# Layer norm on one TensorE-bound core: means, root and reciprocal on 128 columns in four groups of rows, spread by a selector

## The chip, the cores and the metric

The kernel runs on one core of a Trainium2 chip. The core has a matrix engine (TensorE, PE in the profile, with its weight loads as PEld), a vector engine (VectorE, DVE), a scalar engine (ScalarE, ACT), a general engine (GpSimd, POOL) and an engine that issues most of the transfers (SyncE, SP). Each engine works off its own instructions in order and waits on semaphores for the others. The metric is the device time of one execution in microseconds (us), lower being better.

## The reference, cut to what matters

A two-layer network over 1024 latent tokens and 1024 channels. Layer 0 has a convolution branch and a recurrent branch that share one input and one output projection. The convolution branch ends in a layer norm over the channels of each token, a SiLU, and a product with a gate:

```python
def layernorm(x, g, b):
    mu = jnp.mean(xf, axis=-1, keepdims=True)
    var = jnp.mean(jnp.square(xf - mu), axis=-1, keepdims=True)
    y = (xf - mu) * lax.rsqrt(var + LN_EPS) * g + b
...
def conformer_conv(va, vg, p):
    u = va * jax.nn.sigmoid(vg)
    u = depthwise_conv(u, p["conv_w"], p["conv_b"], CONV_PAD)
    return jax.nn.silu(layernorm(u, p["ln_g"], p["ln_b"]))
...
    y_a = conformer_conv(va, vg, p) * jax.nn.silu(ga)
    y_b, hT = rglru_branch(xb, p, h0, True)
    y_b = y_b * jax.nn.silu(gb)
    return jnp.concatenate([y_a, y_b], axis=-1) @ p["w_out"], hT
```

The matrices are float32, and the result is to be near float32.

## The kernel before, in words

Everything is stored transposed: channels on the 128 partitions in 8 tiles (`KT`), tokens along the free dimension in two halves `h` of 512 columns (`H`). A float32 matrix product is made from three products of a reduced format (`F32R`): each operand is split into a high part (a ScalarE cast) and a remainder (a subtraction on VectorE or GpSimd), and high x high, high x low and low x high are added in PSUM. One half of one 128-row weight tile is therefore 8 x 3 = 24 products of 128x128 by 128x512. `mm3_fixed` issues them as eight steps of three.

In layer 0 up to the end of the gate products the order on each engine is written out by hand: `on(engine, ...)` ties every instruction to the one before it on the same engine, through the helpers `act`, `cast` (both ScalarE), `vec` (VectorE) and `gp` (GpSimd). All of these show up in the profile under line 670, so groups are told apart by tile names there. What comes after `fixed[0] = False` is put in order by a planner, by estimated times and priorities.

The part around the change, in program order:

- The convolution runs on VectorE as a generator, whose steps `fill(n)` hands out between other work. `ln_sums` adds each finished channel tile of its result `us[j]` into `lnacc[h]`, so that afterwards only the sum over the 128 partitions is missing.
- The loop over `m` (8 weight tiles of the recurrent branch's output projection, tiles `wob`) issues the 24 products of each half, then the layer norm's work that is due there, then `wob_evict`: a ScalarE scaling out of PSUM, a sum on GpSimd and a store.
- At (m, h) = (6, 0), behind its products, the rest of the convolution is issued, `mean_parts` splits `lnacc` of both halves (128x512), and `mean` multiplies both parts by a 128x128 matrix of 1/1024. That sums over the partitions and leaves the mean `lnmu[h]` on all 128 of them.
- At (6, 1) and (7, 0), behind the products, come the squares of half 0 and of half 1: per channel tile a subtraction of the mean (VectorE), a square (ScalarE) and a sum (VectorE), the sums two tiles behind. After those of half 0 its sum is split (`lnparts`).
- At (7, 1), behind the products, `ln_root(0, ...)` issues two mean products and ScalarE's root on 128x512, and `lnacc` of half 1 is split. `ln_root(1, ...)` follows behind the second half of the first gate tile (`ga`).
- Two gate tiles (`ga_product` for tiles 0 and 4) are four more halves of 24 products. Then, per half, `ga_silu`, `ln_scale` (the reciprocal on 128x512 and eight multiplications on VectorE), eight `ln_silu` on ScalarE and `ga_evict` (the product with the gate).

PSUM: `psum` hands out four banks in turn to the ordinary products; `banks(name, n)` gives the layer norm two further banks for n = 0, and the two halves of one wide tile for n = 1. `ttile` hands out four buffers of 128x512 in turn. `hpool`'s tile `cH` holds half a conditioning vector, which `mod_halves` loads and multiplies with rows of the second layer's modulation.

The second norm of the kernel (layer 1, `row_sums`, `row_spread`, `selector`, tiles `ms_n`, `hl_n`, `rs`) and the first (tiles `ms_x`, `hl_x`, `rx`) work on groups of rows already: four blocks of 128 columns are summed into four groups of 32 partitions.

Of the kernel before, what the change touches and what calls it, by code (L numbers as in the profile page):

```python
# [9 lines left out]
F32 = mybir.dt.float32  # L10
F32R = mybir.dt.float32r
AF = mybir.ActivationFunctionType
# [3 lines left out]
P = 128  # L16
# [4 lines left out]
KT = D // P  # L21
H = 512
HALF = (slice(0, H), slice(H, S))
# [28 lines left out]
def body(ctx, tc, xT, ctxT, cc, ccol, modT, modW, win, gw, wout, wu, grp, wg, wo1, small, edge, ident, outT):  # L52
    nc = tc.nc
    mult, add, sub = ALU.mult, ALU.add, ALU.subtract
# [5 lines left out]
    tpool = ctx.enter_context(tc.tile_pool(name="tpool", bufs=4))  # L60
# [16 lines left out]
    def ttile(name):  # L77
        return tpool.tile([P, H], F32, tag="t", name=name)
# [4 lines left out]
    def psum(name):  # L83
        return pm.tile([P, H], F32, tag="mm", name=name)
# [6 lines left out]
    def banks(name, n):  # L91
        if n % 2:
            t = wide(name)
            return [t[:, h] for h in HALF]
        return [pc.tile([P, H], F32, tag=f"c{i}", name=f"{name}_{i}") for i in range(2)]
# [38 lines left out]
    pe = [None]  # L134
# [39 lines left out]
    def col(o, n=1):  # L174
        return sm[:, o : o + n]

    ones = base.tile([P, P], F32, name="ones")
    nc.vector.memset(ones, 1.0 / D)
    ones_r = base.tile([P, P], F32R, name="ones_r")
# [3 lines left out]
    eps_l = base.tile([P, 1], F32, name="eps_l")  # L183
# [48 lines left out]
    def selector(sel, eng):  # L232
        eng.memset(sel.bitcast(F32), 0.0)
        for i in range(4):
            eng.memset(sel[32 * i : 32 * i + 1, i * P : (i + 1) * P].bitcast(F32), 1.0)
# [61 lines left out]
    with ExitStack() as sctx:  # L297
# [36 lines left out]
        def cast(eng, n, part=slice(0, D)):  # L334
            hi = gs[n[1]][0] if isinstance(n, tuple) else w_tiles(n)[0]
            f = eng.copy if eng is A else lambda o, i: eng.tensor_copy(out=o, in_=i)
            f(hi[:, part], raws[n][:, part])
# [77 lines left out]
        hh, hl = [None] * KT, [None] * KT  # L415
# [95 lines left out]
        parts = tpool.tile([P, 2, 2 * P], F32R, tag="t", name="hl_x")  # L511
# [121 lines left out]
        for i in range(2):  # L633
            v = cx[i].rearrange("p (k n) -> p k n", n=C)
# [31 lines left out]
    def on(eng, f, *args, **kw):  # L666
        with ExitStack() as octx:
            if eng in last:
                octx.enter_context(tc.issue_after(last[eng].ins))
            last[eng] = f(*args, **kw)  # L670
        return last[eng]

    def act(*args, **kw):
        return on("act", nc.scalar.activation, *args, **kw)
# [7 lines left out]
    def mm3_fixed(ps, w, xs, cols):  # L682
        hi, lo = w
        xh, xl = xs
        for k in range(KT):
            kc = slice(k * P, (k + 1) * P)
            on("pe", nc.tensor.matmul, ps, hi[:, kc], xh[k][:, cols], start=(k == 0), stop=False)
            on("pe", nc.tensor.matmul, ps, hi[:, kc], xl[k][:, cols], start=False, stop=False)
            on("pe", nc.tensor.matmul, ps, lo[:, kc], xh[k][:, cols], start=False, stop=(k == KT - 1))
            yield  # L690

    def all_of(steps):
        for _ in steps:
            pass
# [23 lines left out]
    lnacc = [atile("lnsum0"), atile("lnsum1")]  # L718
    fixed = [True]

    def vec(f, **kw):
        return on("vec", f, **kw) if fixed[0] else f(**kw)
# [53 lines left out]
    ended, summed, spread_ = [0], [1], [0]  # L776
    NSPREAD = 5

    def ln_sums():
        for j in range(summed[0], ended[0]):  # L780
            for h in range(2):
                first = us[0][:, HALF[h]] if j == 1 else lnacc[h][:, :H]
                vec(nc.vector.tensor_tensor, out=lnacc[h][:, :H], in0=first, in1=us[j][:, HALF[h]], op=add)
        summed[0] = max(summed[0], ended[0])
# [24 lines left out]
    def fill(n):  # L809
        while n > 0:  # L810
            try:
                next(going[0])
                n -= 1
            except StopIteration:
                if begun[0] >= whole_[0]:
                    return
                going[0] = conv(begun[0])
                begun[0] += 1

    with ExitStack() as actx:  # L820
# [82 lines left out]
        for j in range(KT):  # L903
# [35 lines left out]
            name = "gb0" if final else f"xb{j + 1}"  # L939
# [24 lines left out]
            for h in range(2):  # L964
                ps = psum(f"va{j}_{h}")
# [106 lines left out]

    hpool = ctx.enter_context(tc.tile_pool(name="hpool", bufs=1))
    m1p = hpool.tile([P, 2 * KT, 2], F32, name="m1p")
    cH = hpool.tile([P, H], F32, tag="cH", name="cH")

    def vtile(name):
        return vpool.tile([P, H], F32, tag="v", name=name)
# [175 lines left out]
    def wob_evict(m, h):  # L1254
        v = ttile(f"wo_{m}_{h}")
        act(v, wob_ps[m][h], AF.Identity, scale=m0[:, 0, 2 * KT + m : 2 * KT + m + 1])
        t = vtile(f"xp{m}_{h}")
        nc.sync.dma_start(t, xT[m][:, HALF[h]])
        gp(out=t, in0=t, in1=v, op=add)
        nc.sync.dma_start(x1_part[m][:, HALF[h]], t)  # L1260


    lnmu, lnsq = {}, {}

    def mean_parts(acc_, name):
        hi, lo = [tpool.tile([P, H], F32R, tag="t", name=f"{n}_{name}") for n in ("mh", "ml")]
        cast(hi, acc_)
        vec(nc.vector.tensor_tensor, out=lo, in0=acc_, in1=hi.bitcast(F32), op=sub)
        return hi, lo

    def mean(ps, parts):
        for n, v in enumerate(parts):
            on("pe", nc.tensor.matmul, ps, ones_r, v, start=(n == 0), stop=(n == 1))

    def ln_mean(h, parts):
        lnmu[h], lnsq[h] = banks(f"mu{h}", h)
        mean(lnmu[h], parts)

    lsq = {}

    def ln_square(j, h):
        v = us[j][:, HALF[h]]
        vec(nc.vector.tensor_tensor, out=v, in0=v, in1=lnmu[h], op=sub)
        if j == 0:
            act(lnsq[h], v, AF.Square)
        else:
            lsq[j, h] = ttile(f"lsq{j}_{h}")
            act(lsq[j, h], v, AF.Square)

    def ln_add(j, h):  # L1290
        if j > 0:
            vec(nc.vector.tensor_tensor, out=lnacc[h][:, :H] if j == KT - 1 else lnsq[h],
                in0=lnsq[h], in1=lsq.pop((j, h)), op=add)

    lnrt, lnr = {}, {}

    def ln_root(h, parts):
        ps, lnr[h] = banks(f"ms_ln{h}", h)
        mean(ps, parts)
        lnrt[h] = ttile(f"sq_ln{h}")  # L1300
        act(lnrt[h], ps, AF.Sqrt, bias=eps_l)

    def ln_scale(h):
        vec(nc.vector.reciprocal, out=lnr[h], in_=lnrt[h])
        for j in range(KT):
            v = us[j][:, HALF[h]]
            vec(nc.vector.tensor_tensor, out=v, in0=v, in1=lnr[h], op=mult)

    def ln_silu(j, h):
        v = us[j][:, HALF[h]]  # L1310
        act(v, v, AF.Silu, bias=col(O_L4 + j), scale=col(O_LNG + j))

    wob_ps = {}
    for m in range(KT):
        w = gws[KT + m]
        wob_ps[m] = [psum(f"wob{m}_{h}") for h in range(2)]
        steps = [mm3_fixed(wob_ps[m][h], w, (bh, bl), HALF[h]) for h in range(2)]
        if m == 0:
            for h in range(2):
                for _ in range(KT - 1):  # L1320
                    next(steps[h])
        for h in range(2):
            all_of(steps[h])
            if (m, h) == (KT - 2, 0):
                while ended[0] < KT:
                    fill(1)
                ln_sums()
                for q, parts in enumerate([mean_parts(lnacc[q][:, :H], f"mu{q}") for q in range(2)]):
                    ln_mean(q, parts)
            elif m >= KT - 2:  # L1330
                q = m - KT + 2
                for j in range(KT) if (m, h) != (KT - 1, 1) else ():
                    ln_square(j, q)
                    if j > 1:
                        ln_add(j - 2, q)
                if (m, h) != (KT - 1, 1):
                    for j in (KT - 2, KT - 1):
                        ln_add(j, q)
                    lnparts = mean_parts(lnacc[0][:, :H], "ln0") if q == 0 else lnparts
                else:  # L1340
                    ln_root(0, lnparts)
                    lnparts = mean_parts(lnacc[1][:, :H], "ln1")
            wob_evict(m, h)
            fill(7)
            ln_sums()
        gb_weights(KT + m + 2)
# [4 lines left out]
    def ga_product(j, w, h):  # L1351
        gaps[j, h] = psum(f"ga{j}_{h}")
        all_of(mm3_fixed(gaps[j, h], w, (hh, hl), HALF[h]))
# [7 lines left out]

    for n, j in enumerate((0, KH)):
        for h in range(2):
            ga_product(j, gws[2 * KT + n], h)
            if (n, h) == (0, 1):
                ln_root(1, lnparts)
    for h in range(2):
        ga_silu(0, h)
        ln_scale(h)
        for j in (0, KH, 1, KH + 1, 2, KH + 2, 3, KH + 3):  # L1370
            ln_silu(j, h)
        ga_evict(0, h)
    for h in range(2):
        ga_silu(KH, h)
        ga_evict(KH, h)
    fixed[0] = False


    def mod_halves():
        for q in range(2):  # L1380
# [953 lines left out]
```

## Time and profile before

| | |
|---|---|
| median of 3 runs | 1268.32 us (1267.52 to 1270.27) |
| span of the profiled execution, first to last instruction | 1263.6 us |
| PE busy | 1249.8 us, 99% |
| DVE busy | 1139.3 us, 90% |
| ACT busy | 653.8 us, 52% |
| POOL busy | 295.7 us, 23% |
| mean granted TensorE clock | 0.998 |

The page gives the profiled execution's span, and no total of its own; the median of the runs is 4.7 us above that span. Times in the profile count from the first instruction. A row of a timeline is: start, duration, engine, line, operation, output <- inputs, shape, count, and in brackets how long the engine had been idle and what released it. Consecutive products overlap, so the distance between two starts, not the duration, is what a product costs TensorE. A row of waits is: who <- for whom, us in total, times, longest. A row of a tile's answer has the minimum, median and maximum duration in ns.

### The profile page before, as it was taken

The page shows a single profiled execution, that of the slowest core. Times are in us where ns is not written, and L with a number is a line of the kernel's source. Part 1 is how long each engine was busy: PE and PEld are TensorE (multiplying, and loading weights), DVE is VectorE, ACT ScalarE, POOL GpSimd, SP SyncE. Part 2 cuts the span into 40 slices and gives each one's busy share as a digit, 9 for nine tenths or more (in the row PEclk, how much of TensorE's full clock was granted, in tenths as well). Part 3 has the DMA queues.
Part 4 walks back from the last instruction along what each step waited for, and adds up shares of the span by engine and source line. Part 5 has one row for each costly group of instructions (what it writes and reads, how often), then busy time and mean ns, then how long its engine had stood idle before and what let it go on. Part 6 is the DMA issues. An engine that isn't in the chain of part 4 may idle for free.

```text
span 1263.6 us, 16209 instructions
## 1 busy us (share of the span) xinstructions
PE 1249.8 (99%) x5866; PEld 1035.6 (82%) x5866; DVE 1139.3 (90%) x1746; ACT 653.8 (52%) x952; POOL 295.7 (23%) x176
## 2 busy tenths in 40 slices
PE   9999999999999999999999999999999999999997
PEld 7788888888888888888887878888888888888786
DVE  7799999999999999998978969999899987977975
ACT  8464566656666534237535445744343444644642
POOL 0015364436444547543210023000000000000002
PEclk9999999999999999999999999999999999999999
DMA  9970121112121233442436666344323334759723
GB/s 376 388 254 33 52 65 46 63 43 75 42 84 42 84 119 132 159 150 84 147 112 225 202 206 183 103 136 148 125 94 140 117 125 126 268 199 335 285 71 134
DMA packets 78705, 182.29 MB, mean 144 GB/s; under 512 B 7712, under 2 KB 23328, under 8 KB 78624
## 3 DMA queue, kind: packets, MB, share of 16 engines
q1 hardware_dynamic: 67328, 172.33, 39.8%
q10 hardware_dynamic: 11296, 8.92, 2.2%
q8 instruction: 46, 0.75, 0.2%
q14 instruction: 35, 0.29, 0.1%
HBM read 137.18 MB, written 44.04 MB: 143 GB/s over the span
## 4 chain that ended last, share of the span: by engine, by line
PE 70%; DVE 18%; DMA 7%; issue 2%; ACT 2%; POOL 1%; SPq 0%; POOLq 0%; ACTq 0%; DVEq 0%
PE wob L670 7%; DVE conv L670 5%; PE va L670 5%; PE xb L670 4%; PE vg L670 4%; DVE l L670 3%; PE fold L670 3%; PE g L670 3%; PE qb_v L1153 2%; PE ga L670 2%; PE qb_g L1156 2%; PE ga L161 2%; PE qb_v L1156 2%; PE qb_g L1155 2%; PE qb_g L1153 2%
## 5 line engine op out<-in xcount | busy, mean ns | idle before, releaser
L670 DVE SCALAR_TENSOR_TENSOR conv<-u,sm,conv 128x505 f32<-128x505 f32 (+6 forms) x224 | 153.6, 744 | 1.0
L2045 POOL TENSOR_TENSOR o<-x,rr 128x256 f32<-128x256 f32 (+1 forms) x10 | 9.2, 952 | 448.4 <-ACT rr L2045 448.4
L670 ACT ACTIVATE l<-g,sm 128x512 f32<-128x512 f32 (+1 forms) x96 | 58.7, 619 | 57.7 <-PE g L670 57.0
L670 POOL TENSOR_TENSOR l<-l,l 128x1280 f32<-128x1280 f32 x16 | 47.1, 2967 | 25.6 <-ACT l L670 15.1
L670 PE MATMUL gb<-h0h,wl_gb 128*128 128x512 f32 x128 | 49.9, 390 | 0.4 <-POOL wl_gb L670 0.4
L670 PE MATMUL va<-h0h,wl_va 128*128 128x512 f32 x128 | 49.9, 390 | 0.2 <-DVE wl_va L670 0.2
L98 ACT CAST wq_g<-wr_g 128x512 fp32r<-128x512 f32 x48 | 28.2, 621 | 41.9 <-DMA wr_g<-wg 15.6
L670 PE MATMUL gb<-h0l,wh_gb 128*128 128x512 f32 x128 | 49.8, 389 | 0.0
L670 PE MATMUL gb<-h0h,wh_gb 128*128 128x512 f32 x128 | 49.8, 389 | 0.0
L670 PE MATMUL va<-h0l,wh_va 128*128 128x512 f32 x128 | 49.8, 389 | 0.0
L670 PE MATMUL va<-h0h,wh_va 128*128 128x512 f32 x128 | 49.8, 389 | 0.0
L670 PE MATMUL wob<-ybl,wh_wob 128*128 128x512 f32 x128 | 49.8, 389 | 0.0
L670 PE MATMUL wob<-ybh,wl_wob 128*128 128x512 f32 x128 | 49.8, 389 | 0.0
L670 PE MATMUL wob<-ybh,wh_wob 128*128 128x512 f32 x128 | 49.8, 389 | 0.0
L670 DVE TENSOR_TENSOR_SCAN l<-l,l 128x256 f32<-128x256 f32 (+1 forms) x32 | 48.7, 1521 | 1.1
L670 DVE SCALAR_TENSOR_TENSOR conv<-cL,wsum,conv 128x506 f32<-128x506 f32 (+3 forms) x70 | 48.1, 745 | 0.2
L670 POOL TENSOR_TENSOR l<-l,uc 128x1280 f32<-128x1280 f32 x16 | 47.6, 2999 | 0.0
L98 ACT CAST wq_wo<-wr_wo 128x512 fp32r<-128x512 f32 x48 | 28.6, 620 | 35.5 <-DVE wr_wo L1134 12.4
L98 ACT CAST wq_v<-wr_v 128x512 fp32r<-128x512 f32 x48 | 28.1, 620 | 33.7 <-DMA wr_v<-wfold 16.6
L670 PE MATMUL xb<-h0l,wh_xb 128*128 128x512 f32 x112 | 43.8, 391 | 0.0
L670 PE MATMUL xb<-h0h,wh_xb 128*128 128x512 f32 x112 | 43.8, 391 | 0.0
L670 POOL TENSOR_TENSOR wl_xb<-wr_xb,wh_xb 128x1024 fp32r<-128x1024 f32 x7 | 16.8, 2407 | 114.5 <-ACT wh_xb L670 114.5
(680 smaller groups left out, 4362.5 us busy)
## 6 DMA issues: line engine op xcount, KB each, us to landing
modw<-modW SPq DMA_DIRECT2D x16, 512.0 KB, 10.2
mod<-modT SPq DMA_DIRECT2D x32, 256.0 KB, 3.4
wr_v<-wfold SPq DMA_DIRECT2D x16, 512.0 KB, 4.0
wr_g<-wg SPq DMA_DIRECT2D x16, 512.0 KB, 4.3
wr_wo<-wo SPq DMA_DIRECT2D x16, 512.0 KB, 4.1
mod<-modT SPq DMA_DIRECT2D x14, 512.0 KB, 4.5
y_b<-y SPq DMA_DIRECT2D x24, 256.0 KB, 3.5
y_t<-y SPq DMA_DIRECT2D x24, 256.0 KB, 3.1
```

The source lines that it names most:

```text
L98: return (nc.scalar.copy(hi, src), eng.tensor_tensor(out=lo, in0=src, in1=hi.bitcast(F32), op=sub))
L161: mm(ps, hi[:, kc], xh[k][:, cols], start=(k == 0), stop=False)
L670: last[eng] = f(*args, **kw)
L1153: nc.tensor.matmul(ps, hi, xh[k], start=(first and k == 0), stop=False, skip_group_check=not first)
L1155: nc.tensor.matmul(ps, hi, xl[k], start=False, stop=False, skip_group_check=not first)
L1156: mm = nc.tensor.matmul(ps, lo, xh[k], start=False, stop=(k == KH - 1), skip_group_check=not first)
L2045: tail[eng] = f(*args, **kw)
```

## The change

The layer norm's statistics are kept on 128 columns instead of 512. `row_means` sums block i of 128 columns into partitions 32i to 32i+31 (four f32 products by 32 columns of ones). `row_parts` splits the 128x128 result. `rows_out` multiplies both parts by a selector, `sel_ln`, whose block i has a single row of ones at partition 32i, and so spreads block i to all 128 partitions of columns 128i to 128i+127 (eight products of 128 columns). For the variance the root and the reciprocal are taken on 128x128, before the spread, so the PSUM bank `lnr[h]` receives the reciprocal root itself.

The places move as well. The halves of the products are counted by p = 2m + h from `LN0 = 12`. `ln_within(p)` is issued in the middle of a half's products (after four of eight steps), `ln_behind(p)` after them. The selector sits in the buffer of `cH`, which is allocated again behind it; the selector is written by GpSimd before the loop.

```diff
-    cH = hpool.tile([P, H], F32, tag="cH", name="cH")
+    sel_ln = hpool.tile([P, H], F32R, tag="cH", name="sel_ln")
...
+    selector(sel_ln, Sel())
...
-    def mean(ps, parts):
-        for n, v in enumerate(parts):
-            on("pe", nc.tensor.matmul, ps, ones_r, v, start=(n == 0), stop=(n == 1))
...
+    def row_means(ps, acc_):
+        for i in range(4):
+            on("pe", nc.tensor.matmul, ps[32 * i : 32 * i + 32, :P], ones[:, :32], acc_[:, i * P : (i + 1) * P],
+               start=True, stop=True, skip_group_check=True)
...
+    def row_parts(src, name):
+        hi, lo = [tpool.tile([P, H], F32R, tag="t", name=f"{n}_{name}")[:, :P] for n in ("rh", "rl")]
+        cast(hi, src)
+        vec(nc.vector.tensor_tensor, out=lo, in0=src, in1=hi.bitcast(F32), op=sub)
+        return hi, lo
...
+    def rows_out(ps, parts):
+        for i in range(4):
+            for n, v in enumerate(parts):
+                on("pe", nc.tensor.matmul, ps[:, i * P : (i + 1) * P], sel_ln[:, i * P : (i + 1) * P], v,
+                   start=(i == 0 and n == 0), stop=(n == 1), skip_group_check=True)
...
+    def ln_means():
+        for h in range(2):
+            lnmu[h], lnsq[h] = banks(f"mu{h}", h)
+            row_means(lnsq[h], lnacc[h])
+        for h in range(2):
+            lnparts[h] = row_parts(lnsq[h][:, :P], f"mu{h}")
...
+    def ln_root(h):
         ps, lnr[h] = banks(f"ms_ln{h}", h)
-        mean(ps, parts)
-        lnrt[h] = ttile(f"sq_ln{h}")
-        act(lnrt[h], ps, AF.Sqrt, bias=eps_l)
+        row_means(ps, lnacc[h])
+        rt = ttile(f"sq_ln{h}")[:, :P]
+        act(rt, ps[:, :P], AF.Sqrt, bias=eps_l)
+        vec(nc.vector.reciprocal, out=rt, in_=rt)
+        lnparts[h] = row_parts(rt, f"ln{h}")
 
     def ln_scale(h):
-        vec(nc.vector.reciprocal, out=lnr[h], in_=lnrt[h])
...
+    LN0 = 12
+
+    def ln_within(p):
+        if p == LN0:
+            while ended[0] < KT:
+                fill(1)
+            ln_sums()
+            ln_means()
+        elif p in (LN0 + 3, LN0 + 5):
+            ln_root((p - LN0 - 3) // 2)
+
+    def ln_behind(p):
+        if p == LN0:
+            ln_spread(lnmu)
+        elif p in (LN0 + 1, LN0 + 2):
+            squares(p - LN0 - 1)
+        elif p in (LN0 + 3, LN0 + 5):
+            h = (p - LN0 - 3) // 2
+            rows_out(lnr[h], lnparts[h])
...
         for h in range(2):
+            if m:
+                for _ in range(KH):
+                    next(steps[h])
+            ln_within(2 * m + h)
             all_of(steps[h])
+            ln_behind(2 * m + h)
             wob_evict(m, h)
...
+            p = 2 * KT + 2 * n + h
+            gaps[j, h] = psum(f"ga{j}_{h}")
+            steps = mm3_fixed(gaps[j, h], gws[2 * KT + n], (hh, hl), HALF[h])
+            for _ in range(KH):
+                next(steps)
+            ln_within(p)
+            all_of(steps)
+            ln_behind(p)
```

The squares of the two halves (`squares`) stay behind the products of p = 13 and p = 14. The four gate halves have p = 16 to 19. `ln_scaled(0)` and `ln_scaled(1)` (the scaling and the SiLUs) stay behind all four of them.

More of the change, by code (lines that the diff above doesn't have):

```diff
@@ L1260, in wob_evict, with memset, ln_spread @@
         nc.sync.dma_start(x1_part[m][:, HALF[h]], t)
+    class Sel:
+        def memset(self, *args):
+            on("pool", nc.gpsimd.memset, *args)
+    selector(sel_ln, Sel())
     lnmu, lnsq = {}, {}
[L1265 to L1268, printed above, removed]
-        return hi, lo
-    def mean(ps, parts):
-        for n, v in enumerate(parts):
-            on("pe", nc.tensor.matmul, ps, ones_r, v, start=(n == 0), stop=(n == 1))
-    def ln_mean(h, parts):
-        lnmu[h], lnsq[h] = banks(f"mu{h}", h)
-        mean(lnmu[h], parts)
+    def row_means(ps, acc_):
[6 more added lines that the diff above has]
+        vec(nc.vector.tensor_tensor, out=lo, in0=src, in1=hi.bitcast(F32), op=sub)
+        return hi, lo
+    def rows_out(ps, parts):
[3 more added lines that the diff above has]
+                   start=(i == 0 and n == 0), stop=(n == 1), skip_group_check=True)
+    lnparts = {}
+    def ln_means():
[4 more added lines that the diff above has]
+            lnparts[h] = row_parts(lnsq[h][:, :P], f"mu{h}")
+    def ln_spread(ps):
+        for h in range(2):
+            rows_out(ps[h], lnparts[h])
     lsq = {}
@@ L1293, in ln_add @@
                 in0=lnsq[h], in1=lsq.pop((j, h)), op=add)
-    lnrt, lnr = {}, {}
-    def ln_root(h, parts):
+    lnr = {}
+    def ln_root(h):
         ps, lnr[h] = banks(f"ms_ln{h}", h)
-        mean(ps, parts)
-        lnrt[h] = ttile(f"sq_ln{h}")
-        act(lnrt[h], ps, AF.Sqrt, bias=eps_l)
+        row_means(ps, lnacc[h])
[3 more added lines that the diff above has]
+        lnparts[h] = row_parts(rt, f"ln{h}")
     def ln_scale(h):
-        vec(nc.vector.reciprocal, out=lnr[h], in_=lnrt[h])
         for j in range(KT):
@@ L1311, in ln_silu, with squares, ln_scaled @@
         act(v, v, AF.Silu, bias=col(O_L4 + j), scale=col(O_LNG + j))
+    def squares(h):
+        for j in range(KT):
+            ln_square(j, h)
+            if j > 1:
+                ln_add(j - 2, h)
+        for j in (KT - 2, KT - 1):
+            ln_add(j, h)
+    LN0 = 12
[15 more added lines that the diff above has]
+            rows_out(lnr[h], lnparts[h])
+    def ln_scaled(h):
+        ln_scale(h)
+        for j in (0, KH, 1, KH + 1, 2, KH + 2, 3, KH + 3):
+            ln_silu(j, h)
     wob_ps = {}
@@ L1322, in body @@
         for h in range(2):
+            if m:
+                for _ in range(KH):
+                    next(steps[h])
+            ln_within(2 * m + h)
             all_of(steps[h])
[L1324 to L1342, printed above, removed]
+            ln_behind(2 * m + h)
             wob_evict(m, h)
+            for q in range(2):
+                if 2 * m + h == LN0 + 4 + 2 * q:
+                    ln_scaled(q)
             fill(7)
@@ L1363, in body @@
         for h in range(2):
-            ga_product(j, gws[2 * KT + n], h)
-            if (n, h) == (0, 1):
-                ln_root(1, lnparts)
+            p = 2 * KT + 2 * n + h
[6 more added lines that the diff above has]
+            ln_behind(p)
     for h in range(2):
         ga_silu(0, h)
-        ln_scale(h)
-        for j in (0, KH, 1, KH + 1, 2, KH + 2, 3, KH + 3):
-            ln_silu(j, h)
+        if LN0 + 4 + 2 * h >= 2 * KT:
+            ln_scaled(h)
         ga_evict(0, h)
@@ L1376, in body @@
     fixed[0] = False
+    cH = hpool.tile([P, H], F32, tag="cH", name="cH")
     def mod_halves():
```

## The prediction

> **What bounds the kernel now.** I read the page first (busy shares, then the chain that ended last), then TensorE's own list of waits, then the three engines' timelines from 550 to 610 us, where the layer norm lies.
>
> ```profile
> span 1263.6 us, 16209 instructions
> PE 1249.8 (99%) x5866; PEld 1035.6 (82%) x5866; DVE 1139.3 (90%) x1746; ACT 653.8 (52%) x952; POOL 295.7 (23%) x176
> PEclk9999999999999999999999999999999999999999
> PE 70%; DVE 18%; DMA 7%; issue 2%; ACT 2%; POOL 1%; SPq 0%; POOLq 0%; ACTq 0%; DVEq 0%
> ```
>
> TensorE (PE) is busy for 99% of the span, and in all 40 slices of it at nine tenths or more of the full clock. Its list of waits from 20 to 1240 us opens with these, the only ones of half a microsecond or more:
>
> ```profile
> PE qc_wo L1155 <- DVE y_b22l L99: 0.9, 1, 0.9
> PE qc_woa L1153 <- ACT wq_woa L98: 0.8, 1, 0.8
> PE qb_woa L1153 <- DVE x L1538: 0.5, 1, 0.5
> ```
>
> All three lie behind the layer norm in the code. Together they are 2.2 us, and none stands in the layer norm: its long vector work is hidden behind products. So a lighter VectorE or ScalarE can give back about 2.2 us at most, while what TensorE is given to do, or to wait for, is added to the span. PE's timeline around the old means:
>
> ```profile
> 561.16 0.39 PE L670 MATMUL mu<-mh_mu,ones_r 128*128 128x512 f32 x1
> 561.39 0.39 PE L670 MATMUL mu<-ml_mu,ones_r 128*128 128x512 f32 x1
> ...
> 578.42 0.39 PE L670 MATMUL ms_ln<-mh_ln,ones_r 128*128 128x512 f32 x1
> ...
> 578.88 0.40 PE L670 MATMUL ga<-h0h,wh_ga 128*128 128x512 f32 x1
> ...
> 590.24 0.40 PE L670 MATMUL ga<-h0h,wh_ga 128*128 128x512 f32 x1
> ```
>
> A 512-column product starts every 0.227 us (0.39 is its latency). 24 make one half of a weight tile, 5.44 us: the half that I call p12 (m=6, h=0) ends at 561.16, p15 (m=7, h=1) at 578.42. The two mean products of h=0 then take 0.46 us, to 578.88, and PE goes on: it does not wait for root or reciprocal.
>
> **The change on TensorE.** Eight products by ones, 0.227 us each, go: 1.82 us. In come 16 short f32 sums of 128 columns (`row_means`) and 32 spreading products of 128 columns (`rows_out`). The same kind of sums stands in the second layer, eight of them between two ordinary products:
>
> ```profile
> 749.64 0.39 PE L670 MATMUL fold<-gh,wl_wu 128*128 128x512 f32 x1
> 749.96 0.65 PE L670 MATMUL ms_n<-n1acc,ones 128*32 128x128 f32 x16
> 750.53 0.50 PE L670 MATMUL fold<-gh,wh_wu 128*128 128x512 f32 x1
> 750.87 0.40 PE L670 MATMUL fold<-gl,wh_wu 128*128 128x512 f32 x1
> ```
>
> From 749.64 to 750.87 are 1.23 us where two products alone take 0.45: eight sums cost 0.78 (16 records start within 0.57, about 0.035 apart; the rest goes at entry and exit). The pair of means costs that, each root's four sums about half the 0.57 and the same edges, 0.5. Sums: 0.78 + 2 x 0.5 = 1.8.
>
> No full-width product of 128 columns in this number format is in the trace. The nearest rows are the second layer's spread at 256 columns, and f32 products of one column:
>
> ```profile
> 756.15 1.13 PE L670 MATMUL rs<-hl_n,sel 128*128 128x256 f32 x8
> 757.11 0.39 PE L670 MATMUL fold<-gh,wh_wu 128*128 128x512 f32 x1
> ...
> 1252.98 0.50 PE L2045 MATMUL fin_ms<-ones,fin 128*128 128x1 f32 x4
> 1253.35 0.58 PE L2045 MATMUL fin_ms<-ones,fq 128*128 128x1 f32 x4
> ```
>
> Eight of 256 columns take 0.96, 0.12 each. A straight line from 512 (0.227) through 256 (0.12) gives 0.067 at 128, the lower end. But one column still takes 0.37/4 = 0.093, a floor per weight load. I take 0.10, next to that floor, so 3.2 us for 32. The upper end is the price of true f32:
>
> ```profile
> 1243.07 1.12 PE L2045 MATMUL fin_ms<-dg,ones 128*128 128x512 f32 x2
> ...
> 1244.15 0.28 PE L1155 MATMUL qc_l<-y_b22l,wq_wo 128*128 128x256 f32 x1
> ```
>
> 512 columns took about 1.0 us (1.08 less the one 256-column product between), so 0.25 for 128.
> [...]
>
> Net PE work: 1.8 + 3.2 - 1.8 = **+3.2 us**, all on the path, since nothing covers PE.
>
> **The wait that comes in.** The four-row form puts a longer chain between sums and spread: sums, ScalarE root, reciprocal, cast, VectorE remainder, then the spreading products. In PE's fixed order these stand behind the second half of the same weight tile, 2.72 us of products after the sums. Is that cover enough? For the mean it is: the sums need VectorE's last accumulation,
>
> ```profile
> 554.39 1.29 DVE L670 TENSOR_TENSOR lnsum<-lnsum,u 128x512 f32<-128x512 f32 x2
> ...
> 561.82 2.48 DVE L670 TENSOR_TENSOR u<-u,mu 128x512 f32<-128x512 f32 x4 [0.20 <-PE mu L670]
> ...
> 570.61 0.69 DVE L670 TENSOR_TENSOR lnsum<-mu,lsq 128x512 f32<-128x512 f32 x1
> ...
> 572.59 0.68 DVE L670 TENSOR_TENSOR u<-u,mu 128x512 f32<-128x512 f32 x1
> ...
> 583.70 0.69 DVE L670 TENSOR_TENSOR lnsum<-mu,lsq 128x512 f32<-128x512 f32 x1
> ...
> 586.44 3.35 DVE L670 RECIPROCAL ms_ln<-sq_ln 128x512 f32<-128x512 f32 x1
> ...
> 605.17 0.68 DVE L670 TENSOR_TENSOR u<-u,ga 128x512 f32<-128x512 f32 x1
> ```
>
> done at 555.7, and p12's middle is at 558.4. The spread then starts at 561.16 + 0.78 = 561.9, the first subtraction follows its first eight products: 561.9 + 0.7 + about 0.3 (561.39 to 561.82 was 0.43 with a longer stream) = 562.9, 1.1 later than before. p13 starts at 563.5.
>
> For the root of h=0 it is not. Its ScalarE operations are chained, in program order, behind all squares of **both** halves and the eviction of p14:
>
> ```profile
> 582.09 0.63 ACT L670 ACTIVATE lsq<-u 128x512 f32<-128x512 f32 x1 [0.89 <-DVE u L670]
> 582.62 0.67 ACT L670 ACTIVATE wo<-wob,m 128x512 f32<-128x512 f32 x1
> 583.31 1.28 ACT L670 ACT_TABLE_LOAD   x1
> 584.61 0.69 ACT L670 ACTIVATE sq_ln<-ms_ln,eps_l 128x512 f32<-128x512 f32 x1
> ```
>
> That order was there before; but then only VectorE waited for the root. Now PE does, with every later product queued behind it. VectorE does the squares of h=0 in 9.48 us (561.82 to 571.30), so 562.9 to 572.4. It no longer waits for the cast and remainder that filled 571.30 to 572.59, so the squares of h=1 start 0.2 earlier than before and all rows from 572.59 to 584.61 move up by 0.2: table loaded at 584.4. The small pieces come from these:
>
> ```profile
> L119 ACT ACTIVATE rt_x<-ms_x,eps_r x1: 477/477/477, 26.8 to 26.8; 128x256 f32<-128x256 f32 x1
> L119 DVE RECIPROCAL rt_x<-rt_x x1: 1750/1750/1750, 28.0 to 28.0; 128x256 f32<-128x256 f32 x1
> ...
> L2045 ACT COPY rr<-fin_ms x3: 372/373/588, 1244.2 to 1256.8; 128x256 f32<-128x256 f32 x2, 128x512 f32<-128x512 f32 x1
> ```
>
> Root: 0.69 at 512, 0.477 at 256, so 0.37. Reciprocal: 3.35 and 1.75, so 0.95. Cast: 0.588 and 0.372, so 0.27. With about 0.05 for each handover: 584.8, 585.8, 586.2. PE reaches the spread at 563.5 + 3 x 5.44 + 0.5 = 580.4. **PE stands still for 586.2 - 580.4 = 5.8 us.** The bounds: a pitch of 0.067 makes it 6.1 (PE 0.5 earlier, VectorE 0.3), one of 0.25 makes it 4.6 (PE later by 16 x 0.15 = 2.4, VectorE by 1.2); the ends of the squares give +-0.7.
>
> The root of h=1 waits for nothing old: its squares are done by 584.2. Its chain after the sums is 0.3 + 0.37 + 0.95 + 0.27 + handovers, some 2.1, and 2.4 with the remainder, under the 2.72 of cover. Cost 0, with 0.3 us of room; were the cover gone it would be late by tenths.
>
> **What else moves.** VectorE sheds 2 x 2.4 us of reciprocal and four remainders; it waits for the root of h=1 (about 598), then scales. In before scaling began at 589.8 and the gate product of ga0, h=1 came at 605.17; now about 3 us later, while PE is 9 later, and it needs that buffer at about 615: no new wait. The selector's five memsets on GpSimd have their like in the second layer,
>
> ```profile
> L235 POOL MEMSET sel<- x4: 194/197/199, 724.3 to 725.1; 1x128 f32 x4
> L233 POOL MEMSET sel<- x1: 529/529/529, 723.8 to 723.8; 128x512 f32 x1
> ```
>
> 1.3 us in all, on an engine busy 23% of the span, between remainders and sums that go one after another; later they only delay sums that nobody on PE reads: 0. `cH` now shares its buffer with the selector, so its load, queued on SyncE, cannot go before the last spread (599); the weight loads that may stand behind it are wanted 10 us later than before: 0. The waits listed above: VectorE gains some 6 us on PE, and the 0.8 us wait for prepared weights is likeliest to vanish, the others depend on PE itself. I take -0.9, of 0 to -2.2.
>
> **The clock.** The end of the run is the one place where PE thins out, and the granted clock (column after POOL) falls there:
>
> ```profile
> 1257.00:1258.00 1.00, 0.00 (x0) 0.00 (x0) 0.80 (x3) 0.16 (x1) 0.76 (x2) 0.68 0.41 139
> 1258.00:1259.00 1.00, 0.00 (x0) 0.00 (x0) 1.00 (x4) 0.00 (x0) 1.00 (x2) 0.50 0.00 0
> ```
>
> It halves about 3.7 us after the last dense products (the one-column sums at 1253.35 are followed by almost nothing). 5.8 us of standstill is longer than that. How long it stays halved no row shows: at nothing the cost is 0; at as long as it took to fall, 3.7 us at half rate, it is 1.9. I take 1.0.
> [...]
>
> **Sum.** +3.2 work, +5.8 standstill, +1.0 clock, -0.9 given back: **+9.1 us**. The profiled execution's span would go from 1263.6 to 1272.7. The median of the runs, 1268.32, stands 4.7 above that span (start and end around it), so I predict 1277.4.
>
> **Rivals.** (1) The same standstill with the clock left open: +8.1, 1276.4. For it: nothing before the end lowered the clock to where a slice shows it; against: no standstill before was longer than 1.2 us, and the fall at the end. (2) The 128-column products run at the f32 price, 0.25: the spread of the mean delays VectorE by 8 x 0.15 and the later 16 cost 2.4 more: +12.7, 1281.0. For it: the narrowest in this format seen is 256 columns; against: that one shows no break from the line. (3) No standstill, only work: this needs ScalarE's root within the cover, that is, the squares of h=1 done by about 576. Then +3.2 - 0.9 = +2.3, 1270.6. Against: 11.8 us from 572.59 to 584.39. (4) Not slower: as (3), and 128 columns cost 0.067, so the work is 2.1, and the relieved VectorE removes all 2.2 us of waits: -0.1, 1268.2. It decides only if the remainder of the root is ready by 580.4. The 18% of the chain on VectorE speaks for a gain there; that PE has only 2.2 us of waits to lose speaks against more.
>
> **How the numbers follow.** Chances: forecast 0.50, (1) 0.26, (2) 0.10, (3) 0.08, (4) 0.06. 0.2% is 2.5 us, about what a measurement of this kernel can tell from no change. Forecast, (1) and (2) are slower, and nearly half of (3): 0.89. Same takes the rest of (3) and most of (4): 0.08; faster 0.03. With the standstill the least is +5.3 (0.067 per product, no clock loss, all waits regained, squares 0.7 early), the most +14.3 ((2) with 1.9 for the clock and squares 0.7 late). The range goes a little towards (3): +4.2 to +14.2, 1272.5 to 1282.5, and leaves out (3) and (4).
>
> **What the profile will show.** On PE a gap of 5 to 6 us before the first product that reads the selector for the root of h=0, released by ScalarE's cast, and none before that of h=1; 0.10 us from one spreading product to the next; a clock below 1 just behind the gap; the 0.8 us wait for `wq_woa` gone. I am wrong if that gap is under 2 us, since then only products are added, or if the first subtraction starts after 565, since then the products are dearer.

## The result and the profile after

The changed kernel takes 1281.71 us in the median (1278.89 to 1284.15), the kernel before on the same chip 1267.92 (1267.35 to 1270.27): a ratio of 1.011, 95% interval 1.0091 to 1.013, so slower by some 14 us. The forecast was 1277.4, with a range of 1272.5 to 1282.5. The profiled execution of the changed kernel took 1282.71 us.

The head of its page:

```profile
span 1280.9 us, 16331 instructions
PE 1258.5 (98%) x5922; PEld 1039.6 (81%) x5922; DVE 1131.2 (88%) x1746; ACT 650.3 (51%) x952; POOL 294.1 (23%) x181
PEclk9999999999999999998999999999999999999998
```

VectorE is 8 us lighter and ScalarE 3.5, as the change says, but the span is 17.3 longer. Two digits of the clock's row have dropped to 8: the last, where the run ends, and slice 19 (576 to 608 us), where the layer norm's root lies. TensorE's list of waits, from 20 to 1240 us (total, times, longest):

```profile
PE ms_ln L670 <- ACT rh_ln L670: 5.6, 1, 5.6
PE qac_wo L1156 <- DVE wq_wo L99: 2.4, 2, 1.3
PE qa_wo L1156 <- DVE wq_wo L99: 0.8, 1, 0.8
PE qc_woa L1153 <- ACT wq_woa L98: 0.8, 1, 0.8
PE qa_wo L1153 <- ACT wq_wo L98: 0.7, 1, 0.7
```

A wait of 5.6 us in the layer norm is new and stands first. Of the three waits of before the one for `wq_woa` is still there; those for `wq_wo`, between 1105 and 1171 us, are new. TensorE's timeline shows the mean's sums and spread, then the root of h=0 and what follows it, then the root of h=1:

```profile
557.56 0.39 PE L670 MATMUL wob<-ybh,wl_wob 128*128 128x512 f32 x1
557.88 0.64 PE L670 MATMUL mu<-lnsum,ones 128*32 128x128 f32 x16
...
558.79 0.40 PE L670 MATMUL wob<-ybl,wh_wob 128*128 128x512 f32 x1
...
561.35 0.23 PE L670 MATMUL mu<-rh_mu,sel_ln 128*128 128x128 f32 x1
...
562.98 0.28 PE L670 MATMUL mu<-rl_mu,sel_ln 128*128 128x128 f32 x1
563.09 0.44 PE L670 MATMUL wob<-ybh,wh_wob 128*128 128x512 f32 x1
...
579.87 0.39 PE L670 MATMUL wob<-ybh,wl_wob 128*128 128x512 f32 x1
585.83 0.48 PE L670 MATMUL ms_ln<-rh_ln,sel_ln 128*128 128x128 f32 x1 [5.57 <-ACT rh_ln L670]
...
587.71 0.74 PE L670 MATMUL ga<-h0h,wh_ga 128*128 128x512 f32 x1
588.24 0.63 PE L670 MATMUL ga<-h0l,wh_ga 128*128 128x512 f32 x1
...
591.16 0.39 PE L670 MATMUL ga<-h0h,wl_ga 128*128 128x512 f32 x1
...
600.84 0.23 PE L670 MATMUL ms_ln<-rh_ln,sel_ln 128*128 128x128 f32 x1
...
601.69 0.44 PE L670 MATMUL ga<-h0h,wh_ga 128*128 128x512 f32 x1
```

Read the starts. The mean's 16 spreading products run from 561.35 to 563.09, 0.11 each, and nothing waits before them; nor before the eight at 600.84. Before those at 585.83 TensorE stands for 5.57 us. Then the same eight products take 1.88 us (585.83 to 587.71) where those of h=1 take 0.85, and the eight gate products behind them 3.45 (587.71 to 591.16) where eight at 0.227 take 1.82. The clock explains both (stretch in us, then PE, PEld, DVE, ACT, POOL, granted clock, DMA share, GB/s):

```profile
582.00:584.00 2.00, 0.00 (x0) 0.00 (x0) 1.68 (x3) 1.98 (x3) 1.09 (x1) 1.00 0.00 0
584.00:586.00 2.00, 0.17 (x1) 0.18 (x1) 1.15 (x2) 0.97 (x4) 0.17 (x1) 0.56 0.35 131
586.00:588.00 2.00, 2.00 (x9) 1.96 (x10) 0.10 (x1) 1.29 (x2) 1.56 (x2) 0.50 0.00 0
...
590.00:592.00 2.00, 2.00 (x8) 1.64 (x7) 0.00 (x0) 0.00 (x0) 0.03 (x1) 0.73 0.43 89
```

It falls some four us into the standstill and comes back at about 591, 5 us after the work has. What TensorE waits for is the end of ScalarE's row of work:

```profile
581.57 0.63 ACT L670 ACTIVATE lsq<-u 128x512 f32<-128x512 f32 x1 [0.90 <-DVE u L670]
582.11 0.67 ACT L670 ACTIVATE wo<-wob,m 128x512 f32<-128x512 f32 x1
582.80 1.28 ACT L670 ACT_TABLE_LOAD   x1
584.09 0.37 ACT L670 ACTIVATE sq_ln<-ms_ln,eps_l 128x128 f32<-128x128 f32 x1
585.48 0.30 ACT L670 CAST rh_ln<-sq_ln 128x128 fp32r<-128x128 f32 x1 [1.02 <-DVE sq_ln L670]
```

The sums that the root reads were issued by 577.2; the last squares of h=1, an eviction and the table load stand ahead of it. It is the order and not the load of ScalarE that holds the root back: the last four squares each wait 0.9 to 1.25 us for a subtraction on VectorE, so ScalarE was idle from 577.27 to 578.17, when the sums were there. A root ahead of the squares of h=1 was not tried.

### The profile page after: what moved, and what is told of

Same layout as the page of the kernel before. It is cut to its first block, busy times and chain, and to the rows that moved or that the text cites. A ratio compares the mean times of both kernels' runs of the same rounds, so it can differ in the third digit from the quotient of the medians.

```text
span 1280.9 us, 16331 instructions
## 1 busy us (share of the span) xinstructions
PE 1258.5 (98%) x5922; PEld 1039.6 (81%) x5922; DVE 1131.2 (88%) x1746; ACT 650.3 (51%) x952; POOL 294.1 (23%) x181
## 4 chain that ended last, share of the span: by engine, by line
PE 70%; DVE 13%; DMA 10%; issue 3%; ACT 3%; POOL 0%; SPq 0%; POOLq 0%; DVEq 0%; ACTq 0%
PE gb L670 7%; PE va L670 7%; PE xb L670 6%; PE vg L670 6%; PE wob L670 6%; PE g L670 4%; PE fold L670 3%; PE ga L670 2%; DMA wr_g<-wg 2%; PE ga L162 2%; PE ga L161 2%; PE ga L163 2%; DMA modw<-modW 2%; PE xbc L670 2%; DVE ws L1771 1%
## 5 line engine op out<-in xcount | busy, mean ns | idle before, releaser
L670 PE MATMUL vg<-h0h,wh_vg 128*128 128x512 f32 x112 | 43.6, 389 | 0.0
```

## Experiments

The theory after this profile had three parts: TensorE pays for added products; it stands still because the root comes behind the squares of both halves; the standstill drops the clock. A rival blames the extra time of the last stage on the delay itself (loads that then meet other loads).

To follow a delay along a run I compare, here and below, two rows in each kernel with the same rows before: the second layer's first sums, and the final norm's first sum (the times are first and last start).

```profile
L670 PE MATMUL ms_n<-n1acc,ones x16: 272/273/297, 750.0 to 750.3; 128*32 128x128 f32 x16
...
L2045 PE MATMUL fin_ms<-ones,fin x16: 164/250/250, 1240.7 to 1253.2; 128*128 128x1 f32 x16
```

```profile
L670 PE MATMUL ms_n<-n1acc,ones x16: 272/273/297, 760.9 to 761.2; 128*32 128x128 f32 x16
...
L2095 PE MATMUL fin_ms<-ones,fin x16: 164/250/251, 1257.9 to 1270.4; 128*128 128x1 f32 x16
```

Above stands before, below after: 10.9 us late at 750 us, 17.2 at the end. The last column below is the difference of medians against before on the same chip.

| kernel | late at 750 us | late at 1241 us | medians |
|---|---|---|---|
| after | +10.9 | +17.2 | +13.8 |
| after again (e4) | +11.1 | +14.3 | +11.7 |
| before again (e0) | -0.8 | -0.1 | one time |
| root of h=0 one half later (e1) | +6.5 | +9.6 | +7.5 |
| root of h=0 two halves later, of h=1 one (e5) | +6.3 | +7.0 | +5.6 |
| standstill filled (e2) | +9.4 | +10.5 | +10.2 |
| before, with products added (e3) | +11.2 | +11.4 | +9.2 |
| before, `cH` late (e6) | 0.0 | +2.6 | +1.1 |
| mean alone (e7) | +0.7 | +1.5 | -0.3 |

The two columns of delay compare with one profiled execution of before, which was quicker than the median of before (see the end of the next section). So at 1241 us they stand 1.4 to 3.4 above the medians, save in e2, whose own profiled execution (1275.91 us) was 2.5 quicker than its median. The -0.8 of e0 at 750 us goes with a wait of 0.5 at 736 us that the first profile of before has and e0 has not.

**e1_roots_later**: the root of h=0 inside p = 16 instead of 15; that of h=1 stays inside p = 17, and the squares stay too. The spreads move in the same way (those lines are not printed).

```diff
-        elif p in (LN0 + 3, LN0 + 5):
-            ln_root((p - LN0 - 3) // 2)
+        elif p in (LN0 + 4, LN0 + 5):
+            ln_root(p - LN0 - 4)
...
```

> The changed kernel with both roots issued later: that of h=0 inside p=16 instead of p=15, that of h=1 inside p=17 as it is. Theory (the standstill comes from the root chain of h=0 lying behind the squares of h=1 on ScalarE and VectorE): PE reaches the spread of h=0 at about 585.3, the remainder is ready at 585.8, so the gap of 5.6 us falls to 0.5 or less, the clock stays at 1.00 and the 2.3 us of half-rate products go: about 7.4 us less than the changed kernel, 1274 median, +4 on PE against before up to 610 us. Rival (PE is held later anyway, by the gate products' buffers, because scaling starts no earlier): a new wait of 3 us or more in front of the third gate tile, and 1277 or more.

Measured: 1275.75 us, ratio 1.0064 (1.0049 to 1.0079). The standstill shrank, but not to nothing. TensorE's timeline, then ScalarE's, then the windows:

```profile
585.10 0.39 PE L670 MATMUL ga<-h0h,wl_ga 128*128 128x512 f32 x1
587.12 0.33 PE L670 MATMUL ms_ln<-rh_ln,sel_ln 128*128 128x128 f32 x1 [1.64 <-ACT rh_ln L670]
587.73 0.33 PE L670 MATMUL ms_ln<-rl_ln,sel_ln 128*128 128x128 f32 x1 [0.28 <-DVE rl_ln L670]
```

```profile
583.03 1.05 ACT L670 CAST wh_ga<-wr_ga 128x1024 fp32r<-128x1024 f32 x1
584.09 1.28 ACT L670 ACT_TABLE_LOAD   x1
585.39 0.37 ACT L670 ACTIVATE sq_ln<-ms_ln,eps_l 128x128 f32<-128x128 f32 x1
```

```profile
586.00:588.00 2.00, 0.59 (x3) 0.45 (x4) 1.25 (x2) 0.30 (x1) 1.53 (x1) 1.00 0.35 131
588.00:590.00 2.00, 2.00 (x11) 1.73 (x11) 0.00 (x0) 0.00 (x0) 0.00 (x0) 0.73 0.63 176
590.00:592.00 2.00, 2.00 (x6) 1.55 (x5) 0.00 (x0) 0.00 (x0) 0.00 (x0) 0.50 0.21 86
592.00:594.00 2.00, 2.00 (x15) 1.21 (x15) 0.00 (x0) 0.37 (x1) 0.00 (x0) 0.92 0.00 0
```

The root moved one more place back in ScalarE's order, behind a weight cast of 1.05 us, so it starts 1.3 later than in the changed kernel. And a standstill of only 1.9 us (1.64 and 0.28) still halved the clock (to 0.50), when TensorE was already at work again, for some 3.4 us: eight gate products at 0.43 instead of 0.227, a loss of 1.6 us. The gap shrank to a third, the clock's loss only from 2.3 (e2, below) to 1.6.

**e5_no_gap**: the same edit with `(LN0 + 5, LN0 + 6)` and `ln_root(p - LN0 - 5)`, so the root of h=0 inside p = 17 and that of h=1 inside p = 18.

> The changed kernel with the roots still later, inside p=17 and p=18, so that the ScalarE work that held the root of h=0 back with the root at p=16 (two evictions, a weight cast and the table load, root at 585.4) is over before its sums. Theory: no gap on PE in the layer norm, the clock at 1.00 throughout, and only the added products stay: +3.5 us on PE up to 610 us against before (0.57 + 1.7 + 2 x 0.45 + 2 x 0.9 of sums and spreads with their edges, less 1.8), about 1272 in the median. Rival (the shorter VectorE work starts so late that the next gate products wait for their buffer): no gap at the spreads, but one of 1 us or more before the second half of the third gate tile, +5 or more.

Measured: 1273.44 us, ratio 1.0048 (1.0035 to 1.0061). No gap before the root's spread (first row below) and no lower clock in the layer norm; at 630 us this kernel is 3.6 late, about what the products alone cost. But at 680 us stands a wait that was 0.8 before:

```profile
591.11 0.23 PE L670 MATMUL ms_ln<-rh_ln,sel_ln 128*128 128x128 f32 x1
...
680.64 0.39 PE L1156 MATMUL qa_woa<-ya_b21h,wq_woa 128*128 128x512 f32 x1
683.71 0.69 PE L1153 MATMUL qc_woa<-ya_b22h,wq_woa 128*128 128x512 f32 x1 [2.68 <-ACT wq_woa L98]
```

Its windows show the clock at 0.50 again just behind it:

```profile
682.00:684.00 2.00, 0.29 (x1) 0.33 (x2) 2.00 (x4) 1.02 (x2) 0.00 (x0) 0.95 0.89 280
684.00:686.00 2.00, 2.00 (x6) 1.52 (x6) 2.00 (x5) 2.00 (x5) 0.00 (x0) 0.50 0.66 254
686.00:688.00 2.00, 2.00 (x8) 1.58 (x7) 2.00 (x5) 0.29 (x2) 0.00 (x0) 0.70 0.47 161
```

So nearly half of what removing the standstill gained (from 11.5 to 3.6 late) was lost again 90 us later (from 3.6 to 7.1). Why that cast came late here (DMA engines are busy 0.89 of the time in the first of those windows) was not tried.

**e2_busy_gap**: the changed kernel with 24 idle products of 512 columns (nobody reads what they make), into a bank that the spread then overwrites, ahead of the root's spread for h=0.

```diff
+            for i in range(24 if h == 0 else 0):
+                on("pe", nc.tensor.matmul, lnr[0], ones_r, hh[i % KT][:, HALF[0]], start=True, stop=True)
             rows_out(lnr[h], lnparts[h])
```

> The changed kernel with 24 idle products of 512 columns (5.4 us, into the bank that the spread then overwrites) put in front of the spread of h=0, where PE stands still. Nothing else is changed. Theory (the products behind the gap run at half rate because PE did nothing for 5.6 us): the first product behind the spread starts as before or 0.3 us later, but the spreading products follow at 0.11 instead of 0.21 and the gate products at 0.227 instead of 0.43, the granted clock is 1.00 there, and the time falls by 2 to 2.5 us, to about 1279.5. Rival (they are slow for another reason, such as the selector's weights or operands that land late): the same slow row behind the gap, and 1281.7 or 0.3 more.

TensorE's timeline, and the window behind the spread:

```profile
579.73 5.66 PE L670 MATMUL ms_ln<-h0h,ones_r 128*128 128x512 f32 x24
585.46 0.33 PE L670 MATMUL ms_ln<-rh_ln,sel_ln 128*128 128x128 f32 x1
585.78 0.33 PE L670 MATMUL ms_ln<-rl_ln,sel_ln 128*128 128x128 f32 x1
...
586.62 0.45 PE L670 MATMUL ga<-h0h,wh_ga 128*128 128x512 f32 x1
...
588.49 0.39 PE L670 MATMUL ga<-h0h,wl_ga 128*128 128x512 f32 x1
```

```profile
586.00:588.00 2.00, 2.00 (x13) 1.79 (x13) 0.00 (x0) 0.93 (x1) 1.93 (x2) 1.00 0.00 0
```

Measured: 1278.41 us, ratio 1.0091 (1.0071 to 1.0112). The spread starts within 0.4 us of the same place, so the delay of the root is untouched, but the clock stays at 1.00 and the gate products at 0.23. From the first spreading product to the ninth gate product it takes 3.03 us (585.46 to 588.49), the changed kernel 5.33 (585.83 to 591.16): 2.3 us is what the clock costs there. The delay behind the layer norm, by the starts of the same products, is 8.8 us against 11.5; the other 0.4 of these 2.7 stood before it, since at 557 us e2 is 1.0 ahead of before and the changed kernel 0.7. The medians point the same way with less certainty, since the intervals of the two overlap.

**e3_before_delayed**: the kernel before with 50 such products (11.3 us) ahead of the root's mean for h=0: a delay of the same size, in the same place, without the change.

```diff
     def ln_root(h, parts):
         ps, lnr[h] = banks(f"ms_ln{h}", h)
+        for i in range(50 if h == 0 else 0):
+            on("pe", nc.tensor.matmul, ps, ones_r, hh[i % KT][:, HALF[0]], start=True, stop=True)
         mean(ps, parts)
```

> The kernel before, with 50 idle products (11.3 us) in front of the mean product of the root of h=0, so that PE and, behind the root, ScalarE and VectorE lose 11 us at the same place, with nothing else of the change. The changed kernel lost 11.5 us up to 610 us and 17.2 at the end of the profiled run, 13.8 in the medians. Theory A (the rest behind 800 us is what a shift by 11 us does to transfers and to the vector engine, or plain variation): the same growth in the tail, +13 to +14 in the median, 1281.5. Theory B (the rest belongs to the change, such as the late load of cH): the shift stays 11.3 to the end, 1279.2.

Measured: 1277.41 us, ratio 1.0078 (1.0063 to 1.0093). At 630 us it is 12.1 late, of which 0.7 stood before the added products; at the end it is 11.4 late. A delay alone made no new waits in the last stage of this profile, and the medians (+9.2) show no growth over its size either. The rival falls.

**e0_before_again** and **e4_after_again**: both kernels unchanged, to see how far a profile repeats.

> The kernel before, unchanged, for a second profile of it. If the growth behind 800 us in the changed kernel's profile is variation between executions, this one's starts drift against the first profile by 1 to 3 us behind 800 us, with other waits on PE; if not, they agree within 0.5 us to the end.

> The changed kernel again, for a second profile and more times beside the same runs of before. Theory: the part up to 610 us repeats to 0.3 us (gap 5.6, half clock for 8 to 10 products), while the waits behind 840 us differ from the first profile, with another sum between 0 and 6 us; median 1278 to 1283. Rival (the tail's waits belong to the program): the same waits for wq_wo at the same places, 4 to 6 us again.

Before again took 1265.75 us, after again 1279.49, ratio 1.0097 (1.0083 to 1.0111). The layer norm repeats to 0.3 us: the same first wait. The last stage doesn't: +3.2 us from 750 us to the end where the first profile of the changed kernel had +6.3, from partly other waits. TensorE's list of after again opens:

```profile
PE ms_ln L670 <- ACT rh_ln L670: 5.6, 1, 5.6
PE qac_wo L1156 <- DVE wq_wo L99: 1.9, 3, 1.2
PE qc_wo L1155 <- DVE y_b22l L99: 1.1, 1, 1.1
```

**e6_before_ch_late** and **e7_mean_only** take the change apart. e6 is the kernel before with the selector built in `cH`'s buffer, so that `cH` is loaded late, and one 128-column product by the selector behind the root of h=1 to hold the buffer. e7 is the changed kernel with only the mean in the new form; the root's two products by ones and its 512-column root and reciprocal are those of before, at p = 13, 15 and 17.

> The kernel before, with the selector written into cH's buffer and kept alive by one product of 128 columns behind the root of h=1, so that cH loads late as in the changed kernel; the layer norm itself is the old one. Theory (the late load costs nothing, and the growth behind 800 us in the changed kernel comes from transfers, not from this order): +0.1 to +0.4 us, within the runs of before. Rival (the late load and the order that it brings cost in the tail): +2 us or more, in waits on PE behind 840 us.

> The new form for the mean alone: sums of 128 columns inside p=12 and the spread by the selector, but the roots in the old form (split 512-column sums, two products each, root and reciprocal on 512 columns, at the old places). Theory: the mean's chain has cover, so PE only pays its products: 0.78 + 16 x 0.11 - 0.91 = +1.6 us, no gap, the clock at 1.00, about 1270. Rival (any short chain between sums and spread stops PE): a gap before the first spreading product of the mean and +4 or more.

Both also give other values than the two kernels, from a place that I did not find; I read only their times and traces, and lean on them for nothing large. e6: 1268.94 us, ratio 1.0014 (1.0004 to 1.0024); e7: 1267.53, ratio 1.0002 (0.9991 to 1.0012). The added product of e6 stood 1.0 us for the old root, and e7 came out 2.5 below what was expected. In before a cast on ScalarE went behind the SiLU of `cH` at 450 us, and TensorE's next product started 0.84 behind the one before it, instead of 0.227, for want of the weights that come of it:

```profile
479.05 0.39 PE L670 MATMUL gb<-h0l,wh_gb 128*128 128x512 f32 x1
479.89 0.50 PE L670 MATMUL gb<-h0h,wl_gb 128*128 128x512 f32 x1 [0.45 <-POOL wl_gb L670]
```

That wait is in no kernel with `cH` loaded late, e6 among them, and in all with it early. It is worth about 0.6 us and is the one gain of the change that reached TensorE. In e7 the layer norm is 0.9 late: 1.75 of products for the mean, less the 0.8 that this kernel is ahead of before when it gets there. No version beat before beyond the interval.

## Why the prediction was right, and where its sizes were not

**The sign and the mechanism held.** The forecast said slower, by a standstill before the spread of h=0 and none before that of h=1; both are as told, and the bounds that would have refuted it (a gap under 2 us, a first subtraction after 565, which came at 562.40) are far off. The measured median lies only 0.8 us below the upper end of the range, and the forecast sign that the wait for `wq_woa` would go did not come.

**Products: +3.2 sized, 3.7 measured.** The pair of means' sums: 557.56 to 558.79, less two ordinary products, 0.78 as taken. A root's four sums: 0.56 each (576.56 to 577.57 in the timeline, less 0.45) instead of 0.5. A spreading product paces at 0.11 instead of 0.10, so 32 with their entries cost 3.6. Together 0.78 + 1.12 + 3.6, less 1.82 for the products by ones. e5, which pays hardly anything else in the layer norm, is 3.3 to 3.6 late there; the 0.5 that it was ahead of before when it got there is already in that.
The floor of 0.093 per weight load, next to which 0.10 was taken, was the author's estimate from the one-column rows of before (four in 0.37 us); no run shows that it is one.

**The standstill: 5.8 sized, 5.7 measured.** From the end of the slot at 579.87 (0.23 later) to 585.83. The chain's links are where they were put: table load to 584.1 (forecast 584.4), root 0.37, reciprocal to 585.4, spread at 585.8 (586.2). Both ends of the standstill lie 0.3 to 0.4 early, since the 0.6 gained by the late `cH` stands ahead of them. One thing was left out: the second spreading product needs VectorE's remainder as well, which came 0.3 later (0.32 from the first to the second also in e2, 0.06 for h=1).

**The clock: 1.0 sized, 2.3 measured.** This is the term that was mis-sized. It was taken between 0 and 1.9 because the end of the run showed only the fall. The eight spreading products lost 1.0 (1.88 against 0.85; 0.3 of it is the wait for the remainder) and the eight gate products 1.6 (3.45 against 1.82), and e2 gets 2.3 back by work alone. Rival (1), no clock loss, falls; rival (2), the f32 price of 0.25, falls by the pitch of 0.11; (3) and (4) needed the squares of h=1 done by 576, and the last began at 581.57.

**Given back: -0.9 sized, not found.** Of the waits named, that for `wq_woa` stayed: it is 0.8 in every profile but e5's. The one of before at 736 us is missing in after, which falls there from 11.5 late to 10.9, but before again lacks it too, so the change did not remove it. So the relieved VectorE gave TensorE nothing that shows. Against it stands the growth behind 840 us, +6.3 in one profile and +3.2 in the other. Its cause isn't settled: e3 shows that a delay of this size doesn't make it, e0 that two quick executions of before agree within 0.8 (all its runs spread over 5 us), and the two profiles of after differ in it by 3. From 750 us to the end e5 grows by 0.7, e7 by 0.8, e2 by 1.1 and e1 by 3.1, and e6, which has only the late `cH` and one product of the change, by 2.6. One mark goes with the late `cH`: a wait of `qac_wo` for `wq_wo`, 0.7 to 2.4 us in all, stands in all seven profiles with `cH` late and in none of the three with it early. That the late load makes the growth is not shown by it: the medians of e6 (+1.1) and e7 (-0.3) leave little room. I leave it open.

**The sum.** Behind the layer norm the delay is 3.7 + 5.7 + 0.3 + 2.3 - 0.6 = 11.4 by these terms and 11.5 by the starts, against a forecast there of 10.0; medians lie at +11.7 (e4) and +13.8. The forecast's median missed by 4.3 us: +2.0 from products, clock and standstill with the remainder, -0.6 from `cH`, +0.9 not given back, and the remaining 2.0 is scatter and the unsettled growth, which no run here tells apart. Also the 4.7 us between the profiled span and the median of before was misread as start and end: the own time of a profiled execution is only 1.8 above its span (1282.71 and 1280.9), so that execution of before was some 3 us quicker than the median, and before again (1265.75) nearly as quick.

## What to carry over

Before an operation is made shorter by a longer chain, ask which engine waits for the chain's end: here VectorE had carried the old root off TensorE's path, and the short one put ScalarE's whole queue onto it. Place the consumer by the place of the producer in its own engine's order, and look again after moving it, since that order moves too (e1). On this kernel, which TensorE binds (99% busy in before), a wait cost its length plus the clock: 1.6 us more for standstills of 1.9 and 2.7, 2.3 more for one of 5.6, while those of up to 0.9 in before left it at full speed (1.00 from 20 to 1240 us).

## What the runs showed of the hardware

Behind a standstill of 1.9 us (e1) or 2.7 us (e5) the granted clock was 0.50 for about 3.4 us (by the windows above from 588.9 to 592.3 and from 683.8 to 687.2), some 8 products at 0.43 us instead of 0.227; the fall came when work had already begun again, at once in e5 and 1.8 us later in e1. In the changed kernel, with one of 5.6 us, it was 0.50 from 584.2 to 591.1, twice that time; work had begun again at 585.83, so 5.2 us of it passed at the lower clock. What sets the moment of the fall, and that of the return, no run here shows.

A spreading product of 128 columns in fp32r paced at 0.11 us in the changed kernel, hardly under the 0.12 of one with 256 columns in the second layer of before: from 256 columns to 128 the width hardly set the price here.
